# Low pieces of three w_xo blocks made early and kept in DRAM, and the sums of squares moved off GpSimd

## The chip, the cores and the metric

One core of a Trainium2 chip runs the whole program. The metric is the device time of one execution in microseconds (us); of several runs the median is given.

## The reference

One decoder block in float32: 1024 tokens, width 1024, 256 memory tokens, one layer. Cut to what matters:

```python
h = x
h = h + hybrid_mixer(rmsnorm(h, norm_mix), w_in, ...)     # SSD and GLA branches, merged, @ w_o
h = h + mem_cross_attention(rmsnorm(h, norm_xattn), rmsnorm(mem, norm_mem), w_xq, w_xkv, w_xo)
h = h + swiglu(rmsnorm(h, norm_ffn), w_ffn_in, w_ffn_out)
return rmsnorm(h, norm_final)

def mem_cross_attention(n, m, w_xq, w_xkv, w_xo):          # 4 heads of 256
    q = n @ w_xq ; k, v = split(m @ w_xkv)
    p = softmax(q k^T / 16) ; o = p v
    return o @ w_xo

def swiglu(n, w_ffn_in, w_ffn_out):                        # hidden width 2816
    g, u = split(n @ w_ffn_in)
    return (silu(g) * u) @ w_ffn_out
```

## The kernel before

**Arithmetic.** TensorE (PE) multiplies float32r numbers. Every operand is split in two pieces: ScalarE (ACT) rounds it to the high piece, VectorE (DVE) subtracts that from the operand and leaves the low piece (`split`). A product takes three matmuls: high by high, high by low and low by high. The large matrix products go by a seven-product scheme of 2x2 blocks, named B11, B21, T1, T2, B22, T3, T4; the names with T need sums or differences of blocks on one side or both.

**Stages.** The program is one long instruction list; those named here end it: w_o; the query projection `xq` (about 1053 to 1129 us of the profiled execution); cross attention (about 1129 to 1194); the output projection `xo` with w_xo (its first matmuls beside the last of attention, to about 1263); the FFN's first product in 11 units of 256 hidden columns, each a `gate` and an `up` of 7 products of 12 matmuls (to about 1740); the FFN's second product.

**xo.** `Kept` is its class. Products come in the order B11, B21, T1, T2, B22, T3, T4, each in two halves x of 24 matmuls, so x = 0 and 1 belong to B11, 2 and 3 to B21, 12 and 13 to T4. `prep` makes the pieces of half x three halves ahead: a `ws` tile for the weights (out of `wr`, loaded by SyncE's queue, SP) and another for the attention output (out of `rq`). Each needs an ACT and a DVE instruction of 128x1024. The combinations of the weights themselves (T1, T2, B22, T3) are summed in DRAM, in `xos_d`, by 12 accumulating or plain transfers that GpSimd (POOL) issues while xq and attention run (`weight_sums`). In the loop over attention steps n = 0 to 9, n = 7 and 8 prepare x = 0 and x = 1.

**Squares.** Each output tile of xo (8 row blocks o, two halves h) is evacuated, stored, scaled into `o`, and squared for the RMSNorm ahead of the FFN (`u_xo_stats.take`). The first square of a half is written to `ssum`; the further ones go to a tile `sq`, which `either` lets DVE or POOL add to `ssum`, by a planner's count of each engine's load. After the last square, PE sums over partitions (`close`), `rsqrt` uses DVE for the scaling and POOL for the power, and `rows` spreads the result back over partitions into `ssum`; `gpost` multiplies the hidden tiles by it (instructions `o<-o,ssum`).

**FFN in.** Each `gate` and `up` loads a 1 MB tile `raw`; its T blocks need sums of quarters (`sa`, and `raw<-raw`). Those are made on DVE for units 0 and 1, and for later units by POOL, with the `raw<-raw` of some on DVE, behind POOL's `sa`. POOL's queue also carries `down_d`, the sums in DRAM of the blocks of w_ffn_out.

**What sets the order.** The tile scheduler orders instructions by the order of the code and by `high_priority`; `pinned` keeps an instruction at its place in the program's order. Each engine and each queue runs its list in order, so one that waits holds all behind it. `run` steps one generator beside another, `waiting(g, n)` delays one by n steps.

Of the kernel before, what the change touches and what calls it, by code (L numbers as in the profile page):

```python
# [9 lines left out]
F32 = mybir.dt.float32  # L10
F32R = mybir.dt.float32r
I32 = mybir.dt.int32
AF = mybir.ActivationFunctionType
ALU = mybir.AluOpType
# [64 lines left out]
def block_kernel(ctx: ExitStack, tc: tile.TileContext, t: dict, out: bass.AP):  # L79
# [16 lines left out]
    wp = pool("w", 3)  # L96
    ps = pool("ps", 1, bass.MemoryType.PSUM)

    def dram(name, *shape):
        return dr.tile(list(shape), F32, name=name, tag=name)  # L100

    xT_d = dram("xT_d", D, TOK)
    h1_d = dram("h1_d", D, TOK)
    h2_d = dram("h2_d", D, TOK)
    xqs_d = dram("xqs_d", 2 * D, HALF)
    xos_d = dram("xos_d", 2 * D, HALF)
    xbc_d = dram("xbc_d", 1536, TOK)
    sz_d = dram("sz_d", D, TOK)
    q_d = dram("q_d", 512, TOK)
# [35 lines left out]
    def slot(key, shape=(P, 2, TOK), dt=F32, name="sl"):  # L145
        pl, n = slots[key]
        return pl.tile(list(shape), dt, name=name, tag="sl", bufs=n)
# [80 lines left out]
    def split(src, hi, lo, e=None, neg=False, pin=lambda x: x):  # L228
        if neg:
            pin(ACT.activation(hi, src, AF.Copy, scale=-1.0))  # L230
            pin(DVE.scalar_tensor_tensor(lo, src, -1.0, hi, ALU.mult, ALU.subtract))
        else:
            pin(ACT.activation(hi, src, AF.Copy))  # L233
            pin(sub(e or DVE, lo, src, hi))
# [213 lines left out]
    def run(main, *rest, prio=0):  # L448

        owed = [0.0] * len(rest)  # L450
        for _ in main:
            for i, (g, rate) in enumerate(rest):
                owed[i] += rate
                while owed[i] >= 1.0:
                    owed[i] -= 1.0
                    with tc.high_priority(offset=prio):
                        next(g, None)

    def waiting(g, n):
        for _ in range(n):  # L460
            yield
        for _ in g:
            yield
# [5 lines left out]
    def drain(g):  # L469
        for _ in g:  # L470
            pass
# [18 lines left out]
    def weight_sums(todo):  # L490


        jobs = []
        for A, d, n, k0 in todo:
            put = lambda m, d=d, n=n, k0=k0, kn=A.shape[2]: (
                d[(m * n + k0) * P:(m * n + k0 + kn) * P].rearrange("(k p) c -> p k c", p=P))
            q = {(i, j): A[j][:, :, half(i)] for i in range(2) for j in range(2)}
            jobs.append([(put(0), q[1, 0], 0), (put(2), q[0, 0], 0), (put(0), q[1, 1], 1), (put(2), q[1, 0], 1),
                         (put(1), put(0), 0), (put(3), q[0, 1], 0), (put(1), q[0, 0], 1), (put(3), put(1), 1)])
        for step in zip(*jobs):  # L500
            for o, a, more in step:
                kn = o.shape[1]
                for c in (slice(0, kn // 2), slice(kn // 2, kn)) if more and kn > 3 else (slice(0, kn),):
                    if more:
                        pinned(POOL.dma_start(o[:, c], a[:, c], accum_op=ALU.add))
                    else:
                        pinned(POOL.dma_start(o, a))
                    POOL.t += slower[0]
                    yield
# [5 lines left out]
    class Stats:  # L515
# [3 lines left out]
            s.r = cp.tile([P, NCH], F32, name="rstd", tag="rstd", bufs=2)  # L519
            s.n, s.rest = [0, 0], None  # L520

        def take(s, j, ap, cs=ALL, last=False, e=None):
            dst = s.sum[:, half(j)][:, cs]
            if s.n[j] == 0:
                ACT.activation(dst, ap, AF.Square)
            else:
                q = s.pl.tile([P, HALF], F32, name="sq", tag=s.tag, bufs=s.bufs)[:, cs]
                ACT.activation(q, ap, AF.Square)  # L528
                if last:
                    s.rest = q  # L530
                else:
                    add(e or either(q), dst, dst, q)
            s.n[j] += 1
# [699 lines left out]
    class Wide:  # L1233
# [74 lines left out]
        def prep(s, n, pin=None):  # L1308
            free = lambda x: x
            while len(s.ops) < min(n, 14):  # L1310
                m, kp = divmod(len(s.ops), 2)
                name, c = s.SEQ[m], slice(2 * kp, 2 * kp + 2)
                at = pin or (pinned if len(s.ops) in s.pins else free)
                s.load(name)
                x = [slot("op", (P, 2, 2, HALF), F32R, name="ws") for _ in range(2)]
                with ahead():
                    if name in s.COMB and name not in s.combined:
                        s.combine(name, c, at if s.pins else free)
                    split(s.raw[name][:, c], x[0][:, 0], x[0][:, 1], pin=at)
                    split(s.quad(*s.RIGHT[name])[:, c], x[1][:, 0], x[1][:, 1], neg=name == "T2", pin=at)  # L1320
                if name in ("T1", "T2") and s.PLUS:
                    s.raw[s.SEQ[m + 1]] = s.raw[name]
                    s.plus(s.SEQ[m + 1], 2 * kp)
                s.ops.append(x)

        def combine(s, name, c, pin):
            f, *q = s.COMB[name]
# [62 lines left out]
    class Kept(Stored):  # L1390

        SEQ, FIRST, pins = Wide.SEQ, Wide.FIRST, (2, 3, 4, 5)

        def fetch(s, m, kp):
            x = 2 * m + kp
# [203 lines left out]
    def xq_side():  # L1599
        for _ in range(2):  # L1600
            yield
        s1.close(0)
        s1.close(1)
        DVE.tensor_scalar(xsc, s1.r, XSC, None, ALU.mult)
        yield
        ex1 = cp.tile([P, 1], F32, name="ex1")
        ACT.activation(ex1, xsc[:, :1], AF.Exp, scale=0.0)
        yield

    def kv_side():  # L1610
        for _ in range(2):
            yield
        es = fetch_kv(0)
        for _ in range(9):
            yield
        split_kv(es, pinned)
        yield

    xsums = weight_sums([(t["w_xo"].rearrange("(j k p) c -> j p k c", j=2, p=P), xos_d, 4, 0)])
    run(xq.steps(), (xq_side(), 1.0), (kv_side(), 1.0), (waiting(xsums, 3), 1.0))  # L1620
    drain(xsums)
    u_xo_stats = Stats(rp, "ga", 6)
    o_xo = {}

# [5 lines left out]
    def post_xo(o, h, q, last):  # L1630
        SP.dma_start(h2_d[o * P:(o + 1) * P, half(h)], q)
        ACT.activation(row_xo(o)[:, half(h)], q, AF.Copy, scale=col("norm_ffn", o))
        u_xo_stats.take(h, q)

    xo = Kept(t["w_xo"], post_xo, {"*": "m"},
              {(0, 0): "m", (1, 1): "aux", (0, 1): "aux", (1, 0): "ga"}, h1_d)
    xo.sums_d = xos_d

    class Att:


# [57 lines left out]
    for n in range(len(at) + 2):  # L1699
        a = at[n] if n < len(at) else None  # L1700
        b = at[n - 1] if 0 < n <= len(at) else None
        z = at[n - 2] if n > 1 else None
        if a and a.j == 0 and a.h < 3:
            load_kv(a.h + 1)
        if a:
            a.score(0)
        if b:
            b.turn(0)
        if z:
            z.value()  # L1710
        if b:
            b.turn(1)
        if a:
            a.score(1)
        if n in (3, 4):
            xo.load(xo.SEQ[n - 3])
        if n in (7, 8):
            xo.prep(n - 6)


    rbc2 = u_xo_stats.sum
# [1 line left out]
    for u in range(D_FF // 256):  # L1723
        def gpost(i, j, ap):
            mul(either(ap), ap, ap, rbc2[:, half(j)])
            ACT.activation(ap, ap, AF.Silu)
            mul(either(ap), ap, ap, rbc2[:, half(j)])

        gate = Unit(t["w_ffn_in"], 0, 256 * u, post=gpost, key="aux")
        up = Unit(t["w_ffn_in"], 0, D_FF + 256 * u, key="m")  # L1730

        def upost(i, j, ap, u=u, g=gate, v=up, have=set(), did=set()):

            o = g.q(i, j)
            mul(either(ap), o, o, ap)
            have.add((u, i, j))

            def put(name, src):
                r0 = (CHAIN.index(name) * KP + u) * P
                SP.dma_start(act_d[r0:r0 + P, :], src)  # L1740
                did.add((u, name))

            for name, need, mk in (
                    ("B11", ((0, 0),), None), ("B21", ((1, 0),), None), ("B22", ((1, 1),), None),
                    ("T1", ((0, 1), (0, 0)), lambda: (sub, v.q(0, 1), g.q(0, 0), g.q(0, 1))),
                    ("T2", ((1, 1), "T1"), lambda: (add, v.q(0, 0), g.q(1, 1), v.q(0, 1))),
                    ("T3", ((1, 1), (0, 1)), lambda: (sub, v.q(1, 1), g.q(1, 1), g.q(0, 1))),
                    ("T4", ((1, 0), "T2"), lambda: (sub, v.q(1, 0), v.q(0, 0), g.q(1, 0)))):
                if (u, name) in did or not all((u, x) in did if isinstance(x, str) else (u, *x) in have for x in need):
                    continue  # L1750
                if mk:
                    f, d, x, y = mk()
                    f(either(ap), d, x, y)
                    put(name, d)
                else:
                    put(name, g.q(*need[0]))

        up.post = upost
        if u < 2:
            gate.e = up.e = DVE  # L1760
        gu.append([gate, up])
    B = Operands(lambda: Row(row_xo), 4, order=("B11", "T1", "B21", "B22", "T2", "T3", "T4"))
# [220 lines left out]
```

## Time and profile before

| | before |
|---|---|
| median of 3 runs | 1941.19 us (1937.76 to 1942.55) |
| the profiled execution | 1940.62 us |
| its span, first to last instruction | 1938.6 us |
| mean granted TensorE clock | 0.993 |
| PE busy | 1890.6 us, 98% of the span |
| DVE busy | 1377.1 us, 71% |
| ACT busy | 900.7 us, 46% |
| POOL busy | 491.0 us, 25% |

PE is nearly always busy, so a change of the order can gain only what PE idles or runs at a lower clock. Shares over the span say little of one stage; what PE waits for in the stages that the change touches has to be read from waits, timelines and windows there.

### The profile page before, as it was taken

What the parts mean: (1) busy time and instruction counts of PE and PEld (TensorE: products, weight loads), DVE (VectorE), ACT (ScalarE), POOL (GpSimd) and SP (SyncE); (2) the same over time, 40 slices, a digit from 0 to 9 for tenths busy, and PEclk for the clock granted to TensorE, in tenths of its full rate; (3) what the DMA queues carried; (4) which work ended last, traced back from release to release, by engine and by line L of the source; (5) the groups of instructions that cost most, each with busy time, mean ns of one, the idle gap of its engine ahead of it and who ended that gap; (6) DMA issues with size and microseconds to landing.
All of it is one profiled execution on the core that took longest, in us unless ns stands there. A gap on an engine that the chain in (4) does not pass through costs nothing.

```text
span 1938.6 us, 26040 instructions
## 1 busy us (share of the span) xinstructions
PE 1890.6 (98%) x9632; PEld 1591.7 (82%) x9632; DVE 1377.1 (71%) x2000; ACT 900.7 (46%) x1541; POOL 491.0 (25%) x394
## 2 busy tenths in 40 slices
PE   7999999999999999999999999988999999999998
PEld 7998787888878888788888897876788788888888
DVE  7766879877776755553578777996777777766566
ACT  7534564655553444642146566563233333345243
POOL 0012334345443221001112110244332322230002
PEclk9999999999999999999999999999999999999999
DMA  9433383455553653988764662525665564397463
GB/s 345 142 94 102 131 303 112 147 163 184 184 166 121 203 169 125 333 313 254 190 174 165 183 174 60 206 77 151 175 190 162 143 164 155 95 298 265 159 222 123
DMA packets 242898, 345.22 MB, mean 178 GB/s; under 512 B 16442, under 2 KB 143652, under 8 KB 242772
## 3 DMA queue, kind: packets, MB, share of 16 engines
q1 hardware_dynamic: 223380, 293.23, 44.5%
q0 software_dynamic: 17664, 44.04, 10.8%
q10 hardware_dynamic: 1728, 6.29, 0.8%
q8 instruction: 76, 1.25, 0.3%
q14 instruction: 50, 0.41, 0.1%
HBM read 254.06 MB, written 129.30 MB: 198 GB/s over the span
## 4 chain that ended last, share of the span: by engine, by line
PE 83%; DVE 9%; issue 3%; DMA 2%; ACT 1%; POOL 1%; SPq 0%; POOLq 0%; DVEq 0%; ACTq 0%
PE acc L51 64%; PE bank L51 17%; DVE wlo L73 2%; DVE cv L73 2%; PE bank L55 2%; DVE o L73 1%; DMA raw<-in_w_ffn_in_dram 1%; DVE hs L73 1%; DMA hl<-ys_d 0%; POOL ssum L73 0%; DVE ws L73 0%; POOL o L73 0%; ACT cv L787 0%; DMA vraw<-in_w_in_dram 0%; DVE gy L73 0%
## 5 line engine op out<-in xcount | busy, mean ns | idle before, releaser
L233 ACT ACTIVATE whi<-raw 128x512 fp32r<-128x512 f32 x272 | 169.6, 629 | 271.0 <-PE acc L51 234.5
L73 DVE TENSOR_TENSOR wlo<-raw,whi 128x512 fp32r<-128x512 f32 x272 | 230.2, 855 | 85.8 <-ACT whi L233 85.7
L73 DVE TENSOR_TENSOR o<-acc,o 128x512 f32<-128x512 f32 x244 | 167.1, 685 | 96.7 <-PE acc L51 94.0
L51 PE MATMUL acc<-hl,wd 128*128 128x512 f32 x768 | 174.7, 389 | 1.6 <-ACT wd L233 1.2
L51 PEld LDWEIGHTS acc<-hl,wd 128*128 128x128 f32 x768 | 143.9, 188 | 32.4 <-ACT wd L233 1.7
L51 PE MATMUL acc<-fs 128*128 128x512 f32 (+1 forms) x792 | 155.7, 355 | 0.1
L51 PEld LDWEIGHTS acc<-fs 128*128 128x128 f32 x792 | 130.7, 189 | 20.8 <-issue 0.5
L51 PE MATMUL acc<-ws 128*128 128x512 f32 x576 | 133.8, 390 | 0.6 <-DVE ws L73 0.6
L51 PEld LDWEIGHTS acc<-ws 128*128 128x128 f32 x576 | 107.7, 188 | 23.2 <-DVE ws L73 1.0
L73 DVE TENSOR_TENSOR fs<-fr,fs 128x1024 fp32r<-128x1024 f32 (+1 forms) x78 | 93.0, 1225 | 37.2 <-ACT fs L233 36.9
L233 ACT ACTIVATE fs<-fr 128x1024 fp32r<-128x1024 f32 (+1 forms) x78 | 74.2, 983 | 93.8 <-PE acc L51 27.6
L233 ACT ACTIVATE whi<-sa 128x512 fp32r<-128x512 f32 x96 | 59.9, 628 | 111.5 <-PE acc L51 110.0
L73 POOL TENSOR_TENSOR sa<-raw 128x512 f32<-128x512 f32 x43 | 65.7, 1528 | 152.9 <-DMA raw<-in_w_in_dram 76.0
L51 PE MATMUL bank<-ws 128*128 128x512 f32 x432 | 101.4, 394 | 3.1 <-ACT ws L233 2.8
L51 PEld LDWEIGHTS bank<-ws 128*128 128x128 f32 x432 | 82.0, 190 | 21.0 <-ACT ws L233 3.3
L73 POOL TENSOR_TENSOR raw<-raw,sa 128x512 f32<-128x512 f32 x35 | 45.0, 1287 | 207.0 <-DVE wlo L73 207.0
L73 POOL TENSOR_TENSOR ssum<-ssum,sq 128x512 f32<-128x512 f32 (+1 forms) x23 | 40.4, 1757 | 188.4 <-ACT sq L528 167.2
L51 PE MATMUL acc<-T4h,whi 128*128 128x512 f32 x192 | 77.4, 403 | 9.2 <-DVE o L73 9.1
L51 PE MATMUL acc<-T1h,wlo 128*128 128x512 f32 x192 | 75.9, 396 | 4.4 <-DVE wlo L73 4.4
L51 PE MATMUL acc<-B22h,wlo 128*128 128x512 f32 x192 | 76.0, 396 | 2.8 <-DVE wlo L73 2.8
L51 PE MATMUL acc<-B21h,whi 128*128 128x512 f32 x192 | 75.0, 391 | 2.3 <-ACT whi L233 2.3
L51 PE MATMUL acc<-T1h,whi 128*128 128x512 f32 x192 | 76.9, 401 | 0.4 <-ACT whi L233 0.4
(421 smaller groups left out, 5047.6 us busy)
## 6 DMA issues: line engine op xcount, KB each, us to landing
raw<-in_w_in_dram SPq DMA_DIRECT2D x26, 1024.0 KB, 6.3
raw<-in_w_ffn_in_dram SPq DMA_DIRECT2D x22, 1024.0 KB, 7.6
act_d<-o SPq DMA_DIRECT2D x77, 256.0 KB, 3.0
fr<-act_d SPq DMA_DIRECT2D x35, 512.0 KB, 6.2
down_d<-in_w_ffn_out_dram POOLq DMA_DIRECT2D x18, 768.0 KB, 6.5
fr<-down_d SPq DMA_DIRECT2D x20, 512.0 KB, 3.7
csb<-cs_d SPq DMA_DIRECT2D x15, 512.0 KB, 4.1
fr<-in_w_ffn_out_dram SPq DMA_DIRECT2D x15, 512.0 KB, 3.5
```

The source lines that it names most:

```text
L51: return s.e.matmul(o, x, y, **kw)
L55: return s.e.transpose(o, x, i)
L73: return f(*a, **kw)
L233: pin(ACT.activation(hi, src, AF.Copy))
```

## The change

1. `Kept.CUT` names B11, B21 and T4. A generator `cuts` runs beside the query projection: SP loads the six half blocks of 512 KB anew (`wc`), ACT and DVE split them, SP stores the six low pieces to a new DRAM tensor `xol_d`. Later `weights` loads a low piece into its place by a transfer of POOL's queue, and only the high piece is made by ACT again. So six DVE instructions of 128x1024 (`ws<-wr`) leave xo, and six (`ws<-wc`) come in beside xq, with six more of ACT and 18 transfers of 512 KB.
2. Preparation in the attention loop: x = 0 and 1 at n = 6 and 7 (before 7 and 8), x = 2 at n = 8 between value and turn, and x = 3 at n = 9 ahead of the last value, where these two came with xo's own steps before.
3. Squares: the adds to `ssum` are on DVE (11 of 14), and three of them (o = 1 to 3, h = 0) are accumulating transfers of POOL's queue, SBUF to SBUF. Before, 9 were POOL instructions and 5 DVE's.
4. `gate.e = up.e = DVE` for units 0 to 3 (before 0 and 1): the sums `sa` of units 2 and 3 go from POOL to DVE.

```diff
-    def dram(name, *shape):
-        return dr.tile(list(shape), F32, name=name, tag=name)
+    def dram(name, *shape, dt=F32):
+        return dr.tile(list(shape), dt, name=name, tag=name)
...
+    xol_d = dram("xol_d", 6 * P, 2, HALF)
...
-        def take(s, j, ap, cs=ALL, last=False, e=None):
+        def take(s, j, ap, cs=ALL, last=False, e=None, moved=False):
...
+                elif moved:
+                    pinned(POOL.dma_start(dst, q, accum_op=ALU.add))
                 else:
                     add(e or either(q), dst, dst, q)
...
-                    split(s.raw[name][:, c], x[0][:, 0], x[0][:, 1], pin=at)
+                    s.weights(name, kp, x[0], at)
...
+        def weights(s, name, kp, x, pin):
+            split(s.raw[name][:, 2 * kp:2 * kp + 2], x[:, 0], x[:, 1], pin=pin)
...
+        CUT = ("B11", "B21", "T4")
+
+        def cut(s, name, kp):
+            n = 2 * s.CUT.index(name) + kp
+            return xol_d[n * P:(n + 1) * P]
+
+        def cuts(s):
+            todo = [(name, kp) for name in s.CUT for kp in range(2)]
+            r = x = None
+            for n in range(len(todo) + 2):
+                if x is not None:
+                    pinned(SP.dma_start(s.cut(*todo[n - 2]), x[:, 1].bitcast(F32)))
+                    x = None
+                if r is not None:
+                    x = slot("op", (P, 2, 2, HALF), F32R, name="ws")
+                    split(r, x[:, 0], x[:, 1])
+                    r = None
+                if n < len(todo):
+                    name, kp = todo[n]
+                    r = slot("op", (P, 2, HALF), name="wc")
+                    pinned(SP.dma_start(r, s.block(*s.LEFT[name])[:, 2 * kp:2 * kp + 2]))
+                yield
+
+        def weights(s, name, kp, x, pin):
+            if name not in s.CUT:
+                return super().weights(name, kp, x, pin)
+            pinned(POOL.dma_start(x[:, 1].bitcast(F32), s.cut(name, kp)))
+            pin(ACT.activation(x[:, 0], s.raw[name][:, 2 * kp:2 * kp + 2], AF.Copy))
...
-    run(xq.steps(), (xq_side(), 1.0), (kv_side(), 1.0), (waiting(xsums, 3), 1.0))
+    run(xq.steps(), (xq_side(), 1.0), (kv_side(), 1.0), (waiting(xsums, 3), 1.0), (waiting(xo.cuts(), 4), 1.0))
...
-        u_xo_stats.take(h, q)
+        u_xo_stats.take(h, q, e=DVE, moved=o < 4 and h == 0)
...
+        if n == 9:
+            xo.prep(4)
         if z:
             z.value()
+        if n == 8:
+            xo.prep(3)
...
-        if n in (7, 8):
-            xo.prep(n - 6)
+        if n in (6, 7):
+            xo.prep(n - 5)
...
-        if u < 2:
+        if u < 4:
             gate.e = up.e = DVE
```

On POOL's queue, from the last transfers of the sums of w_xo to the first products with the norm (`ws<-xol_d` is the load of a low piece, `ssum<-sq` an accumulating transfer of a square), before and after as one piece of the difference:

```order
 L73 DMA xos_d<-in_w_xo_dram 128x2x512 x2
 L73 DMA xos_d<-xos_d 128x2x512 x2
-L73 TENSOR_TENSOR ssum<-ssum,sq 128x512 x9
+L73 DMA ws<-xol_d 128x1024 x4
+L73 DMA ssum<-sq 128x512 x3
+L73 DMA ws<-xol_d 128x1024 x2
 L73 TENSOR_TENSOR rstd<-rstd,mhalf 128x4 x2
```

The nine adds are gone from POOL; in their place stand four loads of low pieces (B11 and B21), three accumulating transfers, and the two loads for T4, all of which the queue issues in this order.

On DVE, at the end of attention (`phl` is the low piece of a head's weights, `wk<-acc,wk` and `wk<-bank,wk` evacuate a product of xo, `ws<-rq` is a low piece of the attention output), before:

```order
L73 TENSOR_TENSOR phl<-bank,phl 128x512 x2
L73 SCALAR_TENSOR_TENSOR wk<-acc,wk 128x512
L73 TENSOR_TENSOR rq<-rq 128x1024 x2
L73 TENSOR_TENSOR ws<-wr,ws 128x1024
L73 TENSOR_TENSOR ws<-rq,ws 128x1024
L73 TENSOR_TENSOR ws<-wr,ws 128x1024
L73 TENSOR_TENSOR ws<-rq,ws 128x1024
```

and the same place after:

```order
L73 TENSOR_TENSOR ws<-rq,ws 128x1024
L73 SCALAR_TENSOR_TENSOR wk<-acc,wk 128x512
L73 TENSOR_TENSOR rq<-rq 128x1024
L73 TENSOR_TENSOR phl<-bank,phl 128x512 x2
L73 TENSOR_TENSOR rq<-rq 128x1024
L73 TENSOR_TENSOR ws<-rq,ws 128x1024
L73 TENSOR_TENSOR ws<-wr,ws 128x1024
```

The low pieces of B21 (the four `ws` rows after `rq<-rq` before) have moved: those of the weights to the transfers, those of the attention output ahead of the last `phl`. Further on in the same list, the two `rstd<-bank` of `close` begin 42 instructions after the first evacuation into `ga` (the last product of xo) before, and 57 after.

On POOL again, at units 1 to 4 of the FFN, one piece of the difference (`sa` are the sums of a unit's weight quarters, `down_d` the transfers for w_ffn_out, `o<-o` and `o<-o,ssum` products of hidden tiles):

```order
+L73 TENSOR_TENSOR o<-o,ssum 128x512
 L73 DMA down_d<-in_w_ffn_out_dram 128x3x512 x2
-L73 TENSOR_TENSOR raw<-raw,sa 128x4x128
+L73 TENSOR_TENSOR o<-o 128x512
+L73 DMA down_d<-in_w_ffn_out_dram 128x3x512
+L73 DMA down_d<-down_d 128x3x512
+L73 DMA down_d<-in_w_ffn_out_dram 128x3x512
+L73 TENSOR_TENSOR o<-o 128x512
+L73 DMA down_d<-in_w_ffn_out_dram 128x3x512
+L73 DMA down_d<-down_d 128x3x512
+L73 DMA down_d<-in_w_ffn_out_dram 128x3x512
+L73 TENSOR_TENSOR sa<-raw 128x512
```

The sums of units 2 and 3, which stood between these transfers, are gone, and the first `sa` of POOL is that of unit 4, with three `down_d` right ahead of it.

More of the change, by code (lines that the diff above doesn't have):

```diff
@@ L1617, in kv_side @@
         yield
-    xsums = weight_sums([(t["w_xo"].rearrange("(j k p) c -> j p k c", j=2, p=P), xos_d, 4, 0)])
-    run(xq.steps(), (xq_side(), 1.0), (kv_side(), 1.0), (waiting(xsums, 3), 1.0))
-    drain(xsums)
     u_xo_stats = Stats(rp, "ga", 6)
@@ L1637, in block_kernel @@
     xo.sums_d = xos_d
+    xsums = weight_sums([(t["w_xo"].rearrange("(j k p) c -> j p k c", j=2, p=P), xos_d, 4, 0)])
+    run(xq.steps(), (xq_side(), 1.0), (kv_side(), 1.0), (waiting(xsums, 3), 1.0), (waiting(xo.cuts(), 4), 1.0))
+    drain(xsums)
     class Att:
```

## The prediction

> **What bounds the kernel now.** I read the page first, then what PE waits for from the end of attention to unit 3 of the FFN, the only stretch whose engine work the change alters much, then the waits one by one in the timeline, and last a table of 20 us windows.
>
> ```profile
> span 1938.6 us, 26040 instructions
> PE 1890.6 (98%) x9632; PEld 1591.7 (82%) x9632; DVE 1377.1 (71%) x2000; ACT 900.7 (46%) x1541; POOL 491.0 (25%) x394
> PE 83%; DVE 9%; issue 3%; DMA 2%; ACT 1%; POOL 1%; SPq 0%; POOLq 0%; DVEq 0%; ACTq 0%
> ```
>
> PE is busy 98% of the span, and the chain that ended last is PE's for 83% and DVE's for 9%. No matmul of a product is removed, so all that can be won is idle time of PE and time in which its clock is reduced. The waits of PE from 1060 to 1400 us (in total, times, longest):
>
> ```profile
> PE acc L51 <- DVE o L73: 7.1, 1, 7.1
> PE acc L51 <- DVE wlo L73: 4.4, 2, 2.7
> PE bank L51 <- ACT ws L233: 2.8, 1, 2.8
> PE acc L51 <- ACT whi L233: 2.7, 2, 2.3
> PE acc L51 <- DVE ws L73: 0.6, 1, 0.6
> PE bank L51 <- DVE ws L73: 0.3, 1, 0.3
> ```
>
> These are 17.9 us. I call them A (0.6, the first `ws` of xo), B (2.8 and 0.3, x = 2 of xo), C (2.7 and one `wlo` of 2.7, in unit 0 of the FFN), D (the other `wlo`, 1.7) and E (7.1). In PE's timeline (start, duration, in brackets the idle time ahead of it and what ended it):
>
> ```profile
> 1196.21 1.20 PE L51 MATMUL bank<-ws 128*128 128x512 f32 x4 [2.84 <-ACT ws L233]
> 1275.61 0.52 PE L51 MATMUL acc<-B21h,whi 128*128 128x512 f32 x1 [2.35 <-ACT whi L233]
> 1279.27 0.79 PE L51 MATMUL acc<-T1h,wlo 128*128 128x512 f32 x1 [2.71 <-DVE wlo L73]
> 1302.92 0.39 PE L51 MATMUL acc<-T3h,whi 128*128 128x512 f32 x1
> 1303.15 0.39 PE L51 MATMUL acc<-T3l,whi 128*128 128x512 f32 x1
> 1321.53 0.50 PE L51 MATMUL acc<-T1h,wlo 128*128 128x512 f32 x1 [1.67 <-DVE wlo L73]
> 1359.22 0.80 PE L51 MATMUL acc<-T4h,whi 128*128 128x512 f32 x1 [7.09 <-DVE o L73]
> 1359.81 0.63 PE L51 MATMUL acc<-T4l,whi 128*128 128x512 f32 x1
> 1364.83 0.39 PE L51 MATMUL acc<-B11h,whi 128*128 128x512 f32 x1
> ```
>
> After E a matmul takes 0.63 us where it takes 0.39 elsewhere: the clock is halved until about 1364.5. The windows tell what this costs (columns: length, then PE, PEld, DVE, ACT and POOL busy, the granted clock, the DMA share, GB/s):
>
> ```profile
> 1080.00:1100.00 20.00, 20.00 (x98) 16.82 (x97) 9.30 (x15) 9.08 (x13) 3.59 (x4) 1.00 0.42 138
> 1180.00:1200.00 20.00, 16.91 (x73) 13.23 (x72) 12.81 (x19) 10.30 (x17) 0.00 (x0) 0.94 0.24 89
> 1200.00:1220.00 20.00, 20.00 (x88) 16.54 (x87) 20.00 (x21) 12.89 (x18) 1.29 (x1) 0.98 0.26 88
> 1240.00:1260.00 20.00, 20.00 (x89) 16.54 (x89) 19.38 (x24) 12.64 (x22) 7.40 (x5) 1.00 0.59 196
> 1260.00:1280.00 20.00, 14.60 (x59) 10.73 (x58) 20.00 (x32) 18.00 (x34) 5.62 (x2) 0.90 0.18 67
> 1280.00:1300.00 20.00, 20.00 (x97) 16.76 (x96) 20.00 (x34) 7.06 (x13) 8.17 (x3) 0.93 0.32 106
> 1340.00:1360.00 20.00, 12.91 (x56) 10.41 (x55) 8.25 (x13) 3.77 (x7) 5.77 (x5) 0.86 0.70 129
> 1360.00:1380.00 20.00, 20.00 (x80) 16.30 (x79) 14.29 (x22) 5.28 (x9) 6.08 (x4) 0.88 0.76 239
> ```
>
> A window of 20 us at 0.94 loses 1.2 us of full speed. B: 1.2 + 0.4 = 1.6 us. C: 2.0 + 1.4 = 3.4, which is 6.8 us at half clock; 2.7 of these were the idle `wlo` wait, so 4.1 us of work at half speed, 2.05 lost. E: 2.8 + 2.4 = 5.2, but what counts is the work from 1359.22 to 1364.5, 5.3 us at half speed, 2.65 lost. With their clocks: A 0.6, B 4.7, C 7.5, D 1.7, E 9.7, together 24.2 us, the most that the change can win here. DVE is full from 1200 to 1300 (20.00, 19.38, 20.00, 20.00): A, B and C come from a DVE that is behind.
>
> [...]
>
> **Part 1 and 2, the low pieces and the earlier preparation.**
>
> ```profile
> L73 DVE TENSOR_TENSOR ws<-wr,ws 128x1024 fp32r<-128x1024 f32 x12 | 14.6, 1215 | 1.1 <-ACT ws L233 1.1
> 1155.00 1.14 POOL L73 DMA_DIRECT2D xos_d<-xos_d  x1 [5.33 <-issue]
> 1161.31 1.14 POOL L73 DMA_DIRECT2D xos_d<-xos_d  x1 [5.17 <-PE bank L55]
> xos_d<-in_w_xo_dram POOLq DMA_DIRECT2D x6, 512.0 KB, 6.0
> ```
>
> Removed from DVE: 6 x 1.215 = 7.3 us, two of the six (1.215 each) ahead of 1195, two inside B, two for T4. The pieces of the attention output for B21 (2 x 1.2) move ahead too. What appears beside xq: 7.3 us of DVE, as much again less a little of ACT, and 12 transfers of SP's queue, the waits of whose stores stand ahead of later loads. The window from 1080 has 10.7 us of DVE and 10.9 of ACT free and a DMA share of 0.42, PE there is full: I take 0, with 0 to 2 us for a load of T3 or T4 of xq that comes late behind a store. The work that hides it is xq's matmuls; if that cover is gone, a late load costs PE its delay.
>
> A (0.6) and B (4.7) then go, if the four loads are there. They stand on POOL's queue behind the last transfer for `xos_d`, issued at 1161.31, and follow each other by 1.14 + 5.17 = 6.3 us, as that one followed. The first is issued near 1167.6 and lands by 1173.6 (6.0 us, as the 512 KB rows), the others at 1179.9, 1186.2 and 1192.5. By the new order xo's first matmul moves ahead of some attention matmuls, to about 1172; it wants a low piece by its third matmul, a half of 24 matmuls takes 5.5 us (0.23 from the start of one to the next, 1302.92 to 1303.15), and x = 3 is wanted near 1196.5. So the first load comes 0 to 2 us late and the rest in time. I take +1.0, range 0 to 5 (5: the issues 8 us apart, which other rows of this queue, below, show).
>
> **Part 3, the squares.**
>
> ```profile
> 1253.67 4.77 POOL L73 TENSOR_TENSOR ssum<-ssum,sq 128x512 f32<-128x512 f32 x3 [6.82 <-ACT sq L528]
> 1254.41 2.88 DVE L73 TENSOR_TENSOR o<-o 128x512 f32<-128x512 f32 x2
> 1262.52 0.68 DVE L73 SCALAR_TENSOR_TENSOR ga<-acc,ga 128x512 f32<-128x512 f32 x1
> 1263.12 1.28 DVE L73 TENSOR_TENSOR o<-o 128x512 f32<-128x512 f32 x2
> 1087.34 2.03 POOL L73 TENSOR_TENSOR rstd<-rstd,mhalf 128x4 f32<-128x4 f32 x2 [28.73 <-DVE rstd L73]
> 1289.59 6.88 POOL L73 TENSOR_TENSOR rstd<-rstd,mhalf 128x4 f32<-128x4 f32 x2 [15.14 <-DVE rstd L73]
> ```
>
> While POOL adds squares, two DVE products take 2.88 us instead of 1.28: POOL's adds cost DVE time too. Nine of them at up to 1.6 us less the idle hits are about 7 us of DVE. That goes; six more adds at 0.60 (start to start, 1262.52 to 1263.12) come, 3.6 us, for three transfers take the others. [...]
>
> Up to the end of xo, DVE so loses 4 x 1.215 for weights after 1195, 2.4 moved ahead and about 6 of contention, and gains 1.8: 67 us of work become about 56, for 61 us of matmuls. It is no longer behind when xo ends. But after that the norm's chain stands in a worse place: the first `rstd` of DVE came 42 instructions after the evacuation at 1262.52 and comes 57 after it now, 57 x 0.60 = 34.4 us; POOL's power follows, 6.88 us beside a full DVE, 2.03 where DVE has room (the same pair of xq, at 1087). With the evacuation 6 us earlier (4.4 by A and B, the rest because DVE isn't late) the power ends between 1293 and 1298, and with a microsecond for the spread T3 of unit 0 can start between 1294 and 1299 instead of 1302.92: 4 to 9 us earlier, of which A, B and the lows are 4.3. C so gives between 0 and 4.6; I take 1.5, near the bad end, as DVE is full in that window still. ACT's 18.00 from 1260 to 1280 doesn't change.
>
> D: the DVE order has the product that waits for POOL's `o` behind that `wlo`, not ahead; 1.7 may go or come back a product later. I take 1.0.
>
> **Part 4, the sums of units 2 and 3.** E is this:
>
> ```profile
> 1353.52 0.76 POOL L73 DMA_DIRECT2D down_d<-down_d  x1 [6.54 <-issue]
> 1354.29 1.28 POOL L73 TENSOR_TENSOR sa<-raw 128x512 f32<-128x512 f32 x1
> 1355.60 0.69 DVE L73 TENSOR_TENSOR raw<-raw 128x512 f32<-128x512 f32 x1 [10.75 <-POOL sa L73]
> 1384.17 1.25 POOL L73 DMA_DIRECT2D down_d<-down_d  x1 [6.78 <-issue]
> ```
>
> DVE stood 10.75 us in front of a `raw<-raw` until POOL had made `sa`, and POOL had been held by its own transfers, the last 6.54 us behind the one before; behind DVE's instruction stood the evacuation that PE needed. With `sa` on DVE neither can happen at this place: E goes whole, 9.7. DVE pays four sums of 0.60 in a window where it is busy 8.25 of 20: nothing on the path, unless `raw` itself is late.
>
> But the same pattern is now at unit 4: three `down_d` stand right before POOL's first `sa`, each up to 6.78 + 1.27 = 8 us behind the last, and DVE's `raw<-raw` of that gate waits for it, with evacuations behind. POOL is held by hidden products of unit 3 before that. Along the new order I put the first of the three about 2 us into the unit ahead (an estimate), the others 5 to 6.3 us apart, and `sa` 2 us behind the third issue: 14 to 17 us in. PE wants the evacuated bank some 15 us in, and from `sa` to PE it took 3.6 us in E (1355.6 to 1359.2): 3 to 6 us of wait, with or without a half clock. I take 4.5, range 0 to 9.7.
>
> **Sum**, from the profiled execution's 1940.62 (0.6 under the median of 1941.19, which changes nothing): -0.6 (A), -4.7 (B), +1.0 (loads), -1.5 (C), -1.0 (D), -9.7 (E), +4.5 (unit 4) = -12.0, so 1928.6; I say 1928.
>
> **The rivals.**
> 1. *E returns whole at unit 4.* For it: the same three transfers, the same waiting instruction. Against: one hidden product fewer, and DVE alone reaches its place earlier. -12.0 + 5.2 = -6.8: 1934.
> 2. *Everything goes.* C vanishes since DVE caught up, and unit 4 has its `sa` in time: -24.2, 1916.5. Against: the `rstd` chain above.
> 3. *The change buys little.* The power ends late (1304, DVE's evacuation no earlier), so that T3 starts where it did, and E returns whole: only D, 1939.5.
> 4. *Slower: the loads on POOL's queue are late.* The power took 6.88 us beside a full DVE; if issuing a transfer is slowed likewise, so that loads follow each other by 13.5 us (twice the 6.3) the fourth lands at 1214, 17.6 us after PE wants it, with two half clocks of 1.7: 13.0 (the sum without the loads' term) is used up as soon as the lateness passes 13 us, and here it ends 8 above before, 1948. For it: four in a row on a queue that shows 8 us between issues too. Against: DVE is idle a third of the window from 1180 (12.81). [...]
>
> **Chances.** My forecast 0.42 (its own range 1922 to 1933), rival 1 0.18, rival 2 0.15, rival 3 0.13, rival 4 0.12. A measurement of this kernel tells about 0.3%, 5.8 us, from no change. Faster by more: 0.42 + 0.15 and three quarters of rival 1, 0.70; within it the rest of rival 1 and rival 3, 0.18; slower 0.12. The range of 8 in 10 goes from rival 2 to rival 3: 1917 to 1940; it leaves out rival 4 and some of rival 2.
>
> **What would show it.** In the trace of the changed kernel: no idle PE ahead of x = 2 of xo, and the four low loads landing about 6 us apart from 1173; DVE no longer at 20.00 from 1200 to 1260; POOL's power 25 us or more behind the last product of xo, with PE's waits in unit 0 shrunk, not gone; at gate 2 no wait for `o`, and at gate 4 one of 3 to 6 us, DVE standing before `raw<-raw` for POOL's `sa`. I am wrong if PE waits in xo for a load, if xq gets idle time of PE that it had not, or if the wait at unit 4 is as long as E or absent.

## The result and the profile after

The changed kernel takes 1955.46 us (median of 4, 1954.4 to 1960.14), before 1939.47 (median of 4, 1937.03 to 1942.55). The ratio is 1.0086, 95% interval 1.0063 to 1.0110: slower by about 16 us where I had forecast 12 faster, and above the range. Its profiled execution has a span of 1953.0 us, 14.4 more than before. The page, in its own lines:

```profile
span 1953.0 us, 26090 instructions
PE 1894.3 (97%) x9632; PEld 1592.8 (82%) x9632; DVE 1375.3 (70%) x2016; ACT 906.9 (46%) x1547; POOL 462.0 (24%) x384
PE 75%; DVE 9%; issue 8%; DMA 5%; POOL 2%; ACT 2%; SPq 0%; POOLq 0%; DVEq 0%; ACTq 0%
```

The matmuls are as many as before; the chain that ended last has lost 8 points of PE, and DMA, issuing and POOL have most of them. What PE waits for from 1060 to 1440 us (in total, times, longest; one smaller row left out):

```profile
PE acc L51 <- ACT whi L234: 19.1, 6, 13.4
PE acc L51 <- DMA ws<-xol_d: 5.4, 1, 5.4
PE bank L51 <- DVE phl L73: 1.2, 1, 1.2
PE acc L51 <- DVE wlo L73: 0.8, 2, 0.4
PE acc L51 <- ACT pe L1702: 0.6, 1, 0.6
PE bank L51 <- ACT phl L234: 0.6, 1, 0.6
```

The 7.1 us for `o` are gone, and so are the waits for `ws` made by ACT and DVE. Two new ones are larger: 5.4 for a load of a low piece, and 13.4 for a `whi`. In PE's timeline:

```profile
1179.97 2.07 PE L51 MATMUL acc<-ws 128*128 128x512 f32 x4 [5.45 <-DMA ws<-xol_d]
1201.67 2.76 PE L51 MATMUL bank<-phl,kvhl 128*128 128x512 f32 x6 [1.24 <-DVE phl L73]
1429.47 0.80 PE L51 MATMUL acc<-B11h,whi 128*128 128x512 f32 x1 [13.40 <-ACT whi L234]
1430.07 0.63 PE L51 MATMUL acc<-B11l,whi 128*128 128x512 f32 x1
```

Both kernels have 9632 matmuls, so the start of the one with the same number tells how far the changed kernel is behind at each place (worked out from the two traces; numbers chosen where the two orders agree):

| matmul | place | before | after | behind |
|---|---|---|---|---|
| 5800 | xq | 1101.33 | 1100.63 | -0.7 |
| 6400 | xo, past A and B | 1215.58 | 1222.46 | +6.9 |
| 6800 | FFN, past C | 1311.08 | 1317.34 | +6.3 |
| 7000 | past D and E | 1368.73 | 1364.33 | -4.4 |
| 7200 | ahead of unit 4's wait | 1414.06 | 1411.38 | -2.7 |
| 7400 | past it | 1459.39 | 1472.53 | +13.1 |
| 9000 | FFN out | 1824.57 | 1837.92 | +13.35 |

So 7.6 us were lost at the start of xo where the forecast had 4.3 won, and 15.8 at unit 4 where it had 4.5. D and E gave 10.7, just as forecast. Between 7000 and 7200, 1.7 us came back, 1.26 of it a wait for a `whi` at 1377.53, where the forecast had nothing but the hint that D's 1.7 might come back later.

POOL's queue shows the first loss (start, duration, in brackets the idle time ahead and what ended it):

```profile
1107.37 1.19 POOL L73 DMA_DIRECT2D xos_d<-in_w_xo_dram  x1 [9.38 <-issue]
1131.74 1.15 POOL L73 DMA_DIRECT2D xos_d<-in_w_xo_dram  x1 [8.16 <-issue]
1141.95 0.78 POOL L73 DMA_DIRECT2D xos_d<-xos_d  x1 [9.07 <-issue]
1173.10 1.14 POOL L73 DMA_DIRECT2D xos_d<-xos_d  x1 [4.46 <-issue]
1173.79 2.13 POOL L73 DMA_DIRECT2D ws<-xol_d  x3
```

Three of these sums of w_xo (1107.37, 1131.74 and 1141.95) are issued 9 to 10 us behind the one before; before the change the same three came 5.5, 6.4 and 7.1 us behind. The landing times in the trace say why the sums follow each other so: each is issued some 0.3 us after the one ahead of it has landed, and the one issued at 1097.21 took 9.9 us to land, where its like before took 5.3. A row of before in the same stretch:

```profile
1114.13 1.14 POOL L73 DMA_DIRECT2D xos_d<-in_w_xo_dram  x1 [5.05 <-issue]
```

The last is issued at 1173.1 instead of 1161.3, and the loads come right behind it. The new transfers also hold back what stands behind them in SP's queue. Two of its loads of k, two of v and one of w_xo, issued from 1069 to 1079 before, follow from 1121 to 1124 now. The first of them, before and after:

```profile
1069.27 0.50 SPq L1583 DMA_DIRECT2D ga<-kT_d  x1
1120.96 0.43 SPq L1617 DMA_DIRECT2D ga<-kT_d  x1
```

The chain of sums starts 2.2 us late (1091.53, before 1089.34) and is 8.3 us late by the fifth (1122.44, before 1114.13), beside the new transfers; the other 3.5 of the 11.8 come later, beside these delayed loads (the DMA share from 1120 to 1140 is 1.03, before 0.75). No run here separates the two. The 20 us windows tell of the traffic (columns as in the prediction; the DMA share is the last but one), before:

```profile
1100.00:1120.00 20.00, 20.00 (x90) 16.57 (x89) 17.82 (x23) 10.90 (x15) 3.48 (x3) 1.00 0.57 99
```

and after:

```profile
1080.00:1100.00 20.00, 20.00 (x98) 16.82 (x97) 13.98 (x19) 12.06 (x17) 4.58 (x4) 1.00 0.48 149
1100.00:1120.00 20.00, 20.00 (x90) 16.40 (x89) 17.00 (x21) 14.05 (x17) 2.36 (x2) 1.00 0.87 262
1180.00:1200.00 20.00, 19.42 (x80) 15.62 (x81) 7.89 (x14) 9.89 (x17) 0.00 (x0) 0.88 0.44 167
1420.00:1440.00 20.00, 10.53 (x37) 8.39 (x38) 12.55 (x18) 5.28 (x10) 7.95 (x7) 0.66 0.54 125
```

PE stays full in xq: the twelve transfers cost nothing there, as forecast, but the DMA share from 1100 to 1120 went from 0.57 to 0.87.

The second loss, on POOL and on DVE:

```profile
1373.50 0.76 POOL L73 DMA_DIRECT2D down_d<-in_w_ffn_out_dram  x1
1399.11 1.74 POOL L73 TENSOR_TENSOR o<-o 128x512 f32<-128x512 f32 x1 [24.84 <-issue]
1400.80 1.25 POOL L73 DMA_DIRECT2D down_d<-in_w_ffn_out_dram  x1
1413.70 1.26 POOL L73 DMA_DIRECT2D down_d<-down_d  x1 [11.65 <-DMA down_d<-in_w_ffn_out_dram]
1423.17 0.78 POOL L73 DMA_DIRECT2D down_d<-in_w_ffn_out_dram  x1 [8.21 <-issue]
1423.97 1.28 POOL L73 TENSOR_TENSOR sa<-raw 128x512 f32<-128x512 f32 x1
1425.28 0.69 DVE L73 TENSOR_TENSOR raw<-raw 128x512 f32<-128x512 f32 x1 [16.03 <-POOL sa L73]
```

POOL stood idle for 24.84 us in front of one hidden product, then issued the three transfers 12.9 and 9.5 us apart (the DMA share from 1400 to 1420 is 0.97), then made `sa`. Before, the product at the same place had no transfer between it and `sa`:

```profile
1401.74 1.79 POOL L73 TENSOR_TENSOR o<-o 128x512 f32<-128x512 f32 x1 [8.86 <-DVE o L73]
1411.62 1.29 POOL L73 TENSOR_TENSOR sa<-raw 128x512 f32<-128x512 f32 x1 [8.10 <-DMA raw<-in_w_ffn_in_dram]
```

In the changed kernel DVE waited 16.03 us for `sa`, and behind DVE's instruction stood the `o` products that ACT was to take ahead of the next `whi`.

### The profile page after: what moved, and what is told of

Its sections match the earlier page's. It is cut to its first block, busy times and chain, and to the rows that moved or that the text cites. A ratio compares the mean times of both kernels' runs of the same rounds, so it can differ in the third digit from the quotient of the medians.

```text
span 1953.0 us, 26090 instructions
## 1 busy us (share of the span) xinstructions
PE 1894.3 (97%) x9632; PEld 1592.8 (82%) x9632; DVE 1375.3 (70%) x2016; ACT 906.9 (46%) x1547; POOL 462.0 (24%) x384
## 4 chain that ended last, share of the span: by engine, by line
PE 75%; DVE 9%; issue 8%; DMA 5%; POOL 2%; ACT 2%; SPq 0%; POOLq 0%; DVEq 0%; ACTq 0%
PE acc L51 58%; PE bank L51 15%; DVE wlo L73 2%; DVE cv L73 2%; DVE o L73 1%; PE bank L55 1%; DMA raw<-in_w_ffn_in_dram 1%; DMA zr<-sz_d 1%; DVE hs L73 1%; DMA raw<-in_w_xkv_dram 1%; POOL o L73 1%; DMA down_d<-in_w_ffn_out_dram 1%; POOL xos_d L73 1%; DMA hl<-ys_d 0%; POOL ssum L73 0%
## 5 line engine op out<-in xcount | busy, mean ns | idle before, releaser
L73 DVE TENSOR_TENSOR wlo<-raw,whi 128x512 fp32r<-128x512 f32 x272 | 224.7, 834 | 82.5 <-ACT whi L234 82.3
L73 POOL TENSOR_TENSOR sa<-raw 128x512 f32<-128x512 f32 x39 | 60.8, 1560 | 129.6 <-DMA raw<-in_w_in_dram 72.4
L51 PE MATMUL acc<-B11h,whi 128*128 128x512 f32 x192 | 75.8, 395 | 14.9 <-ACT whi L234 14.9
L51 PE MATMUL acc<-B22h,whi 128*128 128x512 f32 x192 | 76.1, 397 | 1.8 <-ACT whi L234 1.7
L51 PE MATMUL acc<-T3h,whi 128*128 128x512 f32 x192 | 76.2, 397 | 0.2
```

Of the source, the lines that this page charges most:

```text
L51: return s.e.matmul(o, x, y, **kw)
L73: return f(*a, **kw)
```

## The experiments

Each time is a median; the ratio is to the kernel before, timed beside it, with its 95% interval. That kernel's median lay between 1939.5 and 1941.0 from one group of runs to the next, so a difference across groups is good to 1 or 2 us.

**no_cuts**: no stored low pieces, the other parts as changed.

```diff
-        CUT = ("B11", "B21", "T4")
+        CUT = ()
-    run(xq.steps(), ..., (waiting(xsums, 3), 1.0), (waiting(xo.cuts(), 4), 1.0))
+    run(xq.steps(), ..., (waiting(xsums, 3), 1.0))
```

> The changed kernel without the low pieces kept in DRAM (nothing of cuts, no loads of lows; weights split in xo as before), with the earlier preparation, the squares and units 2 and 3 on DVE. Theory: the changed kernel loses in two places that have nothing to do with each other, at xo's first weights, which wait 5.45 us for a load, with half clocks and a second row of small waits behind it (12 us against a kernel that has its weights in time), and at unit 4 (13.4 us idle and some 3 more of half clock). Without the loads the first is gone, the second stays: 1941 to 1946 us, an idle stretch of 10 us or more at unit 4, no wait for a load in xo. Rival: the wait at unit 4 is only there because everything ahead of it came late or because of the transfers' traffic; then it is gone as well and the kernel ends near 1928.

Measured: 1942.37 us, ratio 1.0006 (0.9994 to 1.0018). There is no wait for a load, and unit 4 still has 11.85 us:

```profile
1387.10 1.74 POOL L73 TENSOR_TENSOR o<-o 128x512 f32<-128x512 f32 x1 [24.79 <-issue]
1388.80 1.26 POOL L73 DMA_DIRECT2D down_d<-in_w_ffn_out_dram  x1
1399.14 1.25 POOL L73 DMA_DIRECT2D down_d<-down_d  x1 [9.08 <-issue]
1409.63 0.77 POOL L73 DMA_DIRECT2D down_d<-in_w_ffn_out_dram  x1 [9.24 <-issue]
1410.42 1.28 POOL L73 TENSOR_TENSOR sa<-raw 128x512 f32<-128x512 f32 x1
```

Everything is 12 us earlier and the pattern is the same, 24.79 included. So the loss at unit 4 does not hang on the loads.

**part4**: the kernel before with `if u < 4: gate.e = up.e = DVE`, nothing else.

> The kernel before with part 4 alone (sums of units 2 and 3 on DVE). Theory: the wait E of 7.1 us goes (9.7 with its clock) and a longer one comes at unit 4, since POOL's queue has the same rows ahead of its first sa as in the changed kernel (three transfers behind a hidden product): 1943 to 1948 us. Rival: unit 4 waits 3 to 6 us only, as I had forecast, since nothing ahead is late: 1931 to 1936.

Measured: 1947.22 us, ratio 1.0030 (1.0018 to 1.0043), slower. PE's only wait from 1380 to 1440:

```profile
PE acc L51 <- ACT whi L233: 12.7, 1, 12.7
```

Part 4 alone takes E away (matmul 7200 starts 8.7 us earlier against before than matmul 6800 does) and puts a longer wait at unit 4 (14.7 lost from matmul 7200 to 7600). It is a loss by itself.

**sa_all**: the changed kernel with `if u < 11`.

> The changed kernel with the weight sums of all FFN units on DVE, so that no engine waits for POOL's sums behind the down_d transfers. Theory: the wait at unit 4 is DVE standing in front of POOL's sa, so 15 to 17 us go and the lows' loss stays: 1938 to 1942 us. Rival: POOL is late as such, and the hidden products on its queue (also behind the transfers) hold the act_d stores and then the tiles, so the wait comes back at a later unit: 1948 or more.

Measured: 1941.86 us, ratio 1.0001 (0.9990 to 1.0012): 13.6 us below the changed kernel. With no `sa` left on POOL, its transfers are as late as ever (1402.37, 1414.87, 1424.34), and PE waits 3.0 us at the place of the 13.4. What cost the time was an engine standing in front of POOL, not POOL's lateness.

**hid_dve**: the changed kernel with the hidden products of units 2 and 3 on DVE.

```diff
-            mul(either(ap), o, o, ap)
+            mul(DVE if u in (2, 3) else either(ap), o, o, ap)
...
-                    f(either(ap), d, x, y)
+                    f(DVE if u in (2, 3) else either(ap), d, x, y)
```

> The changed kernel with the hidden products of units 2 and 3 (the FFN's o times o and the differences behind them) on DVE instead of either engine, so that POOL's transfers don't stand behind a product that was ready only at 1399 us. Theory: of the 24.6 us from that product to sa the start is what was late; the transfers are issued some 20 us earlier, sa is in time, and 14 to 17 us go: 1938 to 1942. Rival: the transfers themselves are slow (12.9 and 9.5 us apart, DMA engines full from 1401 on), whoever holds them: sa stays late, 1948 or more.

Measured: 1940.07 us, ratio 0.9994 (0.9980 to 1.0008), 15.4 us below the changed kernel. POOL:

```profile
1375.79 0.76 POOL L73 DMA_DIRECT2D down_d<-in_w_ffn_out_dram  x1
1384.88 1.26 POOL L73 DMA_DIRECT2D down_d<-in_w_ffn_out_dram  x1 [8.33 <-issue]
1393.00 1.24 POOL L73 DMA_DIRECT2D down_d<-down_d  x1 [6.87 <-DMA down_d<-in_w_ffn_out_dram]
1400.79 0.78 POOL L73 DMA_DIRECT2D down_d<-in_w_ffn_out_dram  x1 [6.55 <-issue]
1413.52 1.28 POOL L73 TENSOR_TENSOR sa<-raw 128x512 f32<-128x512 f32 x1 [11.95 <-DMA raw<-in_w_ffn_in_dram]
```

The last of the three is issued by 1401.6, and `sa` now waits for its own `raw`, as before the change; PE's longest wait from 1400 to 1440 is 1.07 us. The transfers are still 8 us apart; what made `sa` late is the hidden product in front of the three.

**one_cut**: one low piece made and stored instead of six, all loads reading it.

```diff
-            n = 2 * s.CUT.index(name) + kp
-            return xol_d[n * P:(n + 1) * P]
+            return xol_d[:P]
-            todo = [(name, kp) for name in s.CUT for kp in range(2)]
+            todo = [("B11", 0)]
```

> The changed kernel with one low piece made and stored beside xq instead of six (one load and one store of 512 KB instead of twelve transfers, one pair of ACT and DVE instructions instead of six), and all six later loads on POOL's queue reading that one piece: what the stored pieces hold is so left out, what the queues do in xo is the same. Theory: the first load was late since the twelve transfers beside xq held up POOL's sums of w_xo (last issue at 1173.1 instead of 1161.3); without them the sums end near 1162, the loads land before 1170, PE waits for none, and 12 us go: 1941 to 1946. [...]

Measured: 1941.34 us, ratio 1.0000 (0.9990 to 1.0009), 14 us below the changed kernel. POOL's queue:

```profile
1128.71 0.79 POOL L73 DMA_DIRECT2D xos_d<-xos_d  x1 [6.14 <-issue]
1161.23 1.14 POOL L73 DMA_DIRECT2D xos_d<-xos_d  x1 [4.98 <-issue]
1161.92 2.14 POOL L73 DMA_DIRECT2D ws<-xol_d  x3
```

The sums end where they ended before and PE waits for nothing from 1060 to 1260. So the traffic of the low pieces (with the pairs of ACT and DVE that go with it, and the loads of SP that it holds back: this run takes out all of them) delays the sums, and POOL's queue as such is fast enough. Matmul 6400 starts 5.9 us earlier against before than matmul 5800: A and B are won when the loads are in time.

**sp_lows**: the changed kernel with the loads on SP's queue (`pinned(SP.dma_start(...))` in `weights`).

> The changed kernel with the six loads of low pieces issued by SP's queue, at the same places of the program, instead of POOL's. Theory: the loads no longer stand behind the sums of w_xo, so the first needs only a free tile and its store, long done: no wait in xo's first product, 8 to 12 us less, 1943 to 1948. Rival: the tile comes free late, or SP's queue, in order too, holds them (or they hold its loads of xos_d and h_d behind them): 1952 or more.

Measured: 1941.72 us, ratio 1.0012 (1.0002 to 1.0021), 1 us better than expected. The sums are late as in the changed kernel (last issue at 1174.82), and still PE doesn't wait for a low piece: what counts is that the loads stood behind the sums. The gain at matmul 6400 is 3.5 us, less than in one_cut, and what the rest goes to is not shown; SP's queue shows the loads from 1135.12 to 1172.98, with the load of `xos_d` behind them, as the rival had it, without harm to PE.

**part2**: the kernel before with the earlier preparation alone (the four lines of `prep`).

> The kernel before with the earlier preparation alone (x = 0 to 3 at n = 6 to 9). Theory: wait B came from the preparation of x = 2 behind the last product of attention, and moving it is enough, no stored low pieces needed: 4 to 6 us less than before, E stays, 1934 to 1937. Rival: DVE has to make four low pieces of weights inside attention and holds the softmax there; PE waits in attention instead: 1939 or more.

Measured: 1937.41 us, ratio 0.9983 (0.9974 to 0.9993). Matmul 6400 is 5.7 us earlier against matmul 5800, so A and B go without any stored piece; C grew by about 2.5 us (matmuls 6400 to 6800), and the median is 2.9 us lower, where 4 to 6 were expected.

**part3**: the kernel before with the squares alone.

> The kernel before with the squares alone (11 adds on DVE, 3 by transfers, none on POOL). Theory: worth nothing by itself, since what DVE wins by POOL's silence it pays in six more adds in a stretch where it is full, and waits C stay: 1938 to 1942. Rival: DVE loses the 6 to 7 us of contention and C shrinks as I had forecast: 1934 to 1937.

Measured: 1938.1 us, ratio 0.9991 (0.9982 to 1.0000): nothing that can be told from no change.

**no_cuts_hid**: parts 2, 3 and 4 with the repair of hid_dve, no stored pieces.

> Earlier preparation, squares on DVE and transfers, sums of units 2 and 3 on DVE, hidden products of units 2 and 3 on DVE, no stored low pieces. Theory: both losses are gone and the gains stay: 5.6 us at the start of xo, 9 at unit 2, some 16 at unit 4 against the run without low pieces (11.85 idle and 5 by the clock, less 1 to 2 that came back): 1926 to 1930. Rival: the two effects don't add, since what is won at unit 4 is lost at the load of raw (unit 4 waits for its DMA when everything is earlier): 1934 to 1938.

Measured: 1927.81 us, ratio 0.9935 (0.9920 to 0.9949). Against no_cuts the repair is worth 14.6 us here as well.

**no_squares**: as no_cuts_hid, with the squares as before (`u_xo_stats.take(h, q)`).

> The kernel before with the earlier preparation, the sums of units 2 and 3 and the hidden products of units 2 and 3 on DVE, squares as before and no stored low pieces. Theory: parts 2 and 4 with the repair carry the whole gain (4 for the preparation, 9 for E): 1926 to 1930, no different from the version with the squares moved (1927.8). Rival: the moved squares are what frees DVE at the start of the FFN: 1932 to 1935.

Measured: 1929.58 us, ratio 0.9945 (0.9932 to 0.9958), not to be told from no_cuts_hid. No gain from part 3 shows.

**sp_hid**: the whole change, with both repairs.

> Both repairs on the whole change: the loads of low pieces on SP's queue, and the hidden products of units 2 and 3 on DVE. Theory: the two losses add, so do their repairs; against the run with SP loads alone (matmuls from unit 5 on 0.7 us later than before) unit 4's 12.8 us idle and 3 to 5 by the clock go and 1 to 2 come back: 1925 to 1929, at or 1 to 2 us under the version without stored low pieces (1927.8), since these take 4 x 1.2 us from DVE in xo. Rival: the twelve transfers beside xq and the late sums of w_xo cost as much as the low pieces save: 1929 to 1932, above it.

Measured: 1925.2 us, ratio 0.9929 (0.9915 to 0.9942), the fastest of all. PE's waits from 1060 to 1440:

```profile
PE acc L51 <- ACT whi L234: 5.1, 5, 1.9
PE acc L51 <- DVE wlo L73: 0.4, 1, 0.4
PE bank L51 <- ACT rq L1729: 0.3, 1, 0.3
PE bank L51 <- DVE phl L73: 0.2, 1, 0.2
```

The two losses add: from the changed kernel's median of 1955.5 the one repair gave 13.7, the other 15.4, both together 30.3. Whether the stored low pieces are worth anything stays open: against no_cuts_hid they make 2.6 us of medians, and the two intervals overlap nearly wholly.

## Why the prediction was wrong

**The load term (+1.0, range 0 to 5) is the first step that failed.** Its queue was right, its arithmetic began at the wrong time. I timed the loads from the last sum's issue at 1161.31, as before, while two paragraphs up I let twelve new transfers of 512 KB run beside those sums and costed them for xq's matmuls alone. They moved that issue by 11.8 us. The spacing was wrong too, the other way: I had 6.3 us between loads, from a row of accumulating transfers, each of which was issued some 0.3 us after the one ahead had landed (1161.31 after 1161.00); three plain loads are issued within 2.13 us. The time to land was right: the first took 6.1 us in the trace (forecast 6.0). What the forecast called 0 to 2 us late was 5.45 us. Measured from matmul 5800 to 6400, A, B and the loads cost 7.6 instead of giving 4.3. one_cut, in which the same loads stand in the same queue without that traffic, gives 5.9 there. Of the 13.5 us between the two, 5.45 are the wait itself; its half clock (6.83 us in the record, 4.85 of them with work) takes 2.4; two waits for `phl` of 1.8 together, which one_cut doesn't have, are followed by a second half clock of 3.41 us, 1.7 more. The other 2 us I have not followed.

**The unit 4 term (+4.5, range 0 to 9.7) is the second.** The mechanism was the one named: three transfers ahead of POOL's first `sa`, DVE in front of `raw<-raw`. The size was not: 15.8 us, 13.4 of idle time and 2.3 for the 4.5 us of work at half clock behind it (1429.47 to 1434.0 in the record). I put the first transfer about 2 us into the unit ahead, an estimate with no row behind it; the order shows a hidden product right in front of it, which I had called "held by hidden products" and not priced. By the code that product reads a block of its unit's `up`, and POOL stood idle 24.8 us ahead of it (the profile names no releaser). And I took 5 to 6.3 us between transfers in a stretch whose DMA share came to 0.97 (1400 to 1420): 12.9 and 9.5 were measured, 8 in hid_dve. Before the change POOL's own `sa` for units 2 and 3 stood between the transfers, and from 1300 on nine transfers were issued ahead of the product at 1401.74; in the changed kernel only six were ahead of the one at 1399.11, and three stood behind it. That part 4 alone does this, part4 shows.

**What held.** E went whole: matmuls 6800 to 7000 give 10.7, forecast D and E 10.7. The two `rstd` came where counted: 57 instructions of 0.60 after the evacuation are 34.2 (the forecast's 34.4 is a slip), the trace has 1265.98 to 1300.29, 34.3:

```profile
1265.98 0.68 DVE L73 SCALAR_TENSOR_TENSOR ga<-acc,ga 128x512 f32<-128x512 f32 x1
1300.53 2.40 POOL L73 TENSOR_TENSOR rstd<-rstd,mhalf 128x4 f32<-128x4 f32 x2 [56.07 <-DVE rstd L73]
```

C gave 0.6 (forecast 1.5), though the power took 2.40 us, not 6.88; DVE is still busy for the whole of 1220 to 1240 and 1260 to 1300. DVE's loss beside POOL's adds went, as forecast: the products `o<-o` from 1200 to 1300 have a mean of 682 ns, before 882 (first row before, the other two after):

```profile
L73 DVE TENSOR_TENSOR o<-o 128x512 f32<-128x512 f32 x16 | 13.6, 882 | 0.0
L73 DVE TENSOR_TENSOR o<-o 128x512 f32<-128x512 f32 x16 | 10.6, 682 | 0.0
L73 DVE TENSOR_TENSOR ssum<-ssum,sq 128x512 f32<-128x512 f32 x11 | 7.5, 682 | 0.0
```

And it bought nothing that part3 or no_squares can tell from no change. By these rows the silence of POOL gives 16 x 0.20 = 3.2 us on the products, and six more adds of DVE (11, before 5) take 6 x 0.68 = 4.1; that this is why nothing is left is worked out, not tested.

**The rivals.** Rival 4 had the right sign and the place of the first loss (late loads), with the wrong reason: it let POOL's issuing be slowed beside a full DVE, which no run here shows. Three loads were issued in 2.13 us (DVE was busy 8.52 of the 20 us from 1160), and with the traffic gone they were in time on the same queue (one_cut, three in 2.14). Its 1.7 for a half clock has no row in the forecast; in the trace before, the one behind B lasts 3.41 us at a granted clock of 0.50, which loses 1.7. Rival 1 had the place of the second loss and stopped at E's size. I had made them exclusive, and both came.

## What to carry to other kernels

Transfers that hide well under one engine can still delay others that share the DMA engines, as the last sum of w_xo here (issued at 1173.10, in one_cut at 1161.23): ask of each added transfer which chain of dependent transfers runs beside it, what stands behind it in its own queue, and who stands behind that chain's last. In a queue that runs in order, the time of an instruction is set by the latest thing ahead of it (`sa` at 1423.97 stood behind a hidden product at 1399.11 and three transfers), so price the instruction right in front of the one that matters, above all one that waits for an engine's result; taking easy work out of a queue can move a late one to the head. When a wait goes because its work moved, look for the next place with the same three rows in the order: here it was two units later and twice as long.

## What the runs showed of the hardware that I had not expected

- POOL issued plain loads much faster than chained sums: three of 512 KB in 2.13 us, against 5 to 13 us between links of a chain of sums. In the chain of w_xo each link was issued some 0.3 us after the one ahead had landed (1131.74 after 1131.42, 1141.95 after 1141.62).
- The chained transfers were farther apart with more traffic beside them: about 6 us at a DMA share of 0.57 (1100 to 1120, before), 6 to 10 at 0.87 (the same window of the changed kernel).
- Two waits of 0.58 and 1.24 us within 4 us were followed by 3.41 us of half clock (window 1200 to 1220 of the changed kernel: 0.91), while D's 1.67 was not, and a wait of the same 1.67 us in unit 0 of the changed kernel was (3.41 us from 1294.05). Less than 2 us in all went ahead of it here:

```profile
1200.00:1220.00 20.00, 18.76 (x76) 14.97 (x75) 15.64 (x17) 13.77 (x19) 0.88 (x1) 0.91 0.17 48
```

- In the traces before and after, from 60 to 1900 us, the starts of the half-clock stretches lie whole multiples of 3.413 us apart (1197.46, 1275.96 and 1354.47 before; 1177.99, 1201.89, 1294.05 and 1420.34 after). Counted in intervals of that length between such starts, PE was idle for 1.82 us in the one that holds the pair, and for 1.76 in that of unit 0's wait of 1.67 (small gaps included); D's wait is cut in two and leaves 1.19. In these two traces each interval with 1.76 us or more was followed by half clock, and none at full clock with less was (1.46 at the most). That the 1.7 us of the second half clock above may be absent from another run of the same kernel is an estimate from these numbers, not shown.
